# Half of a 31-tap depthwise convolution moved from the vector engine to float32 matmuls with diagonal matrices, in a two-block transformer kernel

## The chip, the cores and the metric

The kernel runs on one core of one Trainium2 chip. A core has five engines that work side by side and wait for each other by semaphores: TensorE (PE, with its weight loads PEld), VectorE (DVE), ScalarE (ACT), GpSimd (POOL) and SyncE (SP), which issues most of the transfers. The metric is the device time of one execution in microseconds (us); lower is better. Each engine takes its instructions strictly in the order in which they stand in its own list.

## The reference

The input is one sequence of 256 positions with 1024 channels, all in float32. A first block has two layers. Each layer has a hybrid mixer and a feed-forward part; the first layer's is dense, the second layer's is a mixture of 8 experts of which 2 are used per position. A second block (grouped attention, a linear recurrence and a dense feed-forward) follows. The part that the change touches is the convolution branch of the hybrid mixer:

```python
def hybrid_mixer(x, cos, sin, lambda_init, w_in, w_o, conv_dw, conv_dw_b, conv_ln_g, conv_ln_b, conv_pw, ...):
    proj = x @ w_in
    p_conv, p_q, p_k, p_v, p_dn, p_z, p_b, p_a = split_projection(proj)
    c_lin, c_gate = jnp.split(p_conv, 2, axis=-1)
    c = c_lin * jax.nn.sigmoid(c_gate)
    c = depthwise_conv(c, conv_dw) + conv_dw_b      # 256 channels, 31 taps, centred
    c = jax.nn.silu(layer_norm(c, conv_ln_g, conv_ln_b))
    y_conv = c @ conv_pw
    ...
    y_diff = differential_attention(...)            # 4 heads, two softmax maps each
    y_dn = gated_deltanet_bidir(...)                # chunked delta rule, both directions
    return jnp.concatenate([y_conv, y_diff, y_dn], axis=-1) @ w_o
```

The 256 convolution channels lie as two halves of 128, one channel per partition, with the 256 positions along the free axis.

## The kernel before, in words

The work comes in this order, with times read from the profiled execution: mixer of layer 0 (0 to about 226 us), dense feed-forward of layer 0 (226 to 405), mixer of layer 1 (405 to about 650), mixture of experts (650 to about 1600), second block (1600 to the end). Within a mixer, four generators (convolution `c`, attention `a`, delta rule `d`, gates `g`) are stepped in the order of a string (`ORDER`); a tile scheduler then sets the order of each engine's list from that and from its own dependency rules, so an edit in one generator can shift instructions of the others.

Large matmuls are done in three passes: a weight tile `raw` is cast by ACT to a high part `wH` (L173), the rest `wL = raw - wH` is made by DVE or POOL (L175), and PE multiplies three combinations (L179, L180, L181). Smaller matmuls run directly in float32.

Weights come in by `load` (L158): 2 MB into a `raw` buffer of 16 KB per partition. Outside the mixture `RAWS` such buffers are used in turn, from the pool `wp`, so a load waits until the tile that was last in its buffer has been split to the end. In the mixture there are `RAWS` buffers in `wp` and `MORE` in the mixture's own pool `mp`, whose memory the mixer uses before; a buffer in `mp` can be loaded only when the mixer's tiles there are done.

In the convolution branch, `cp` is the padded input of both halves (float32, tag `cv`), `tw` the 31 taps of a half (one per channel) and `acc` the result. For each half ACT makes the centre tap with the bias (L851), and DVE adds the 30 others, one instruction of 128x256 for each tap (L855), each reading and writing `acc`. The branch that has GpSimd in it is not taken, since `TAPS` is 2 and there are two halves. Later, L871 to L894 make the branch's layer norm and its pointwise projection; L871 is a float32 matmul of 128x128 by 128x256.

Other lines that the text names: L510 and L514 (ACT and DVE, the short convolution of the delta rule, tile `cq`), L518 (its silu, DVE), L562 (DVE, product of the delta rule's matrices, needs L557 of PE), L737 and L750 (PE, the delta rule's solve), L231 (ACT copies out of PSUM), L917 to L922 (DVE, rotary embedding), L946 (PE, attention scores), L950 to L963 (softmax), L185 (PE, transposes), L894 (PE, pointwise projection of the convolution branch).

Of the kernel before, what the change touches and what calls it, by code (L numbers as in the profile page):

```python
# [13 lines left out]
AF = mybir.ActivationFunctionType  # L14
OP = mybir.AluOpType
# [5 lines left out]
P = 128  # L21
# [1 line left out]

ORDER = ("ddggddddcaadacgadadaacdadd", "ddggdcddddaagadaacaacdddad")
PATS = (("G", "G", "", "G", "VVG", "VG"), ("VG", "", "G", "G", "VG", "G"))
TAPS = 2

STEPS = "R mb E B3 RT ET bk kd qd szg rot0 rot1 vv pT qdT wT qkT Q2 oc".split()
ENGS = ("VVVGGVGVGGAAAAAAAAA", "VGVVVVVGGGAAAAAAVVA")
# [8 lines left out]

WIDE = 192

MORE = 3
RAWS = 4
KT = D // P
ALPHA = 4.0 ** 0.25
LN_EPS = 1e-5
# [61 lines left out]
class K:  # L107
    def __init__(self, tc, ctx, a):
# [9 lines left out]

        self.raws = [(self.wp, RAWS)]
        self.cst = []  # L120
# [704 lines left out]
    def conv_branch(self, raw, xH, xL, pp, yH, yL, layer):  # L825
        V, A, G, T = self.V, self.A, self.G, self.T
        cb = []
        raw = raw()
        for u in range(2):
            b = self.bank()  # L830
            self.proj_T2(b, raw[:, :, u * 256:u * 256 + 256], xH, xL, pat=PATS[layer][4])
            cb.append(b.rearrange("p (j s) -> p j s", j=2))
        w, wb, g, lb = pp[:, 0:62], pp[:, 62:64], pp[:, 64:66], pp[:, 66:68]
        cv = lambda n=512: self.wk(n, "cv", 3).rearrange("p (j s) -> p j s", j=2)

        hg = self.sm([P, 4], "hg", 1)
        G.tensor_scalar(w, w, 0.5, None, op0=OP.mult)
        G.tensor_scalar(hg, pp[:, 64:68], 0.5, None, op0=OP.mult)
        pw = pp[:, 98:610].rearrange("p (k f) -> p k f", k=2)
        G.tensor_scalar(pw, pw, 0.5, None, op0=OP.mult)  # L840
        th = cv()
        A.activation(th, cb[1], AF.Tanh, scale=0.5)
        cp = cv(572)
        G.memset(cp, 0.0)
        V.scalar_tensor_tensor(cp[:, :, 15:271], th, 1.0, cb[0], op0=OP.add, op1=OP.mult)
        acc = cv()
        yield
        prod = self.wk(1024, "t32", 1).rearrange("p (k s) -> p k s", k=4)
        for j in range(2):
            tw = w[:, j * 31:j * 31 + 31]  # L850
            A.activation(acc[:, j], cp[:, j, 15:271], AF.Identity, scale=tw[:, 15:16], bias=wb[:, j:j + 1])  # L851
            if j < TAPS:
                for k in range(31):
                    if k != 15:
                        V.scalar_tensor_tensor(acc[:, j], cp[:, j, k:k + 256], tw[:, k:k + 1], acc[:, j], op0=OP.mult, op1=OP.add)  # L855
            else:
                for k0, n in ((0, 4), (4, 4), (8, 4), (12, 3), (16, 4), (20, 4), (24, 4), (28, 3)):

                    win = cp[:, j, k0:k0 + 256]
                    win = bass.AP(tensor=win.tensor, offset=win.offset, ap=[win.ap[0], [1, n], [1, 256]])  # L860
                    G.tensor_tensor(prod[:, :n], win, tw[:, k0:k0 + n, None].to_broadcast([P, n, 256]), OP.mult)
                    while n > 1:
                        h = n // 2
                        G.tensor_tensor(prod[:, :h], prod[:, :h], prod[:, n - h:n], OP.add)
                        n -= h
                    G.tensor_tensor(acc[:, j], acc[:, j], prod[:, 0], OP.add)
        yield

        b = self.bank()
        for j in range(2):  # L870
            T.matmul(b[:, 0:256], lhsT=self.c("ones"), rhs=acc[:, j], start=j == 0, stop=j == 1)  # L871
        V.scalar_tensor_tensor(acc, b[:, None, 0:256].to_broadcast([P, 2, 256]), -1.0 / 256, acc, op0=OP.mult, op1=OP.add)
        sq = cv()
        A.activation(sq, acc, AF.Square)
        for t in range(2):
            for j in range(2):
                T.matmul(b[:, t:t + 1], lhsT=sq[:, j, t * P:(t + 1) * P], rhs=self.c("ones")[:, 0:1], start=j == 0, stop=j == 1)
        rs = self.sm([P, 2], "crs", 1)
        V.tensor_copy(rs, b[:, 0:2])
        self.rsqrt(rs, rs, 1.0 / 256, LN_EPS)  # L880
        dg = self.wk(256, "cv", 3)
        for t in range(2):
            ts = slice(t * P, (t + 1) * P)
            V.tensor_scalar(dg[:, ts], self.c("ident"), rs[:, t:t + 1], None, op0=OP.mult)
            T.matmul(b[:, ts], lhsT=self.c("ones"), rhs=dg[:, ts], start=True, stop=True)
        V.tensor_tensor(acc, acc, b[:, None, 0:256].to_broadcast([P, 2, 256]), OP.mult)
        th, u = cv(), cv()
        for j in range(2):
            A.activation(th[:, j], acc[:, j], AF.Tanh, scale=hg[:, j:j + 1], bias=hg[:, 2 + j:3 + j])
            A.activation(u[:, j], acc[:, j], AF.Identity, scale=g[:, j:j + 1], bias=lb[:, j:j + 1])  # L890
        V.scalar_tensor_tensor(u, th, 1.0, u, op0=OP.add, op1=OP.mult)
        for f in range(2):
            for k in range(2):
                T.matmul(b[:, f * 256:f * 256 + 256], lhsT=pw[:, k, f * P:(f + 1) * P], rhs=u[:, k], start=k == 0, stop=k == 1)  # L894
        v = b.rearrange("p (f s) -> p f s", f=2)
        self.split(v, None, yH[:, 0:2], yL[:, 0:2])
# [467 lines left out]
    def moe(self, xn):  # L1364
# [3 lines left out]
        self.raws = [p.tile([P, 4096], F32, tag="raw", name=f"raw{n}x{i}", bufs=n) for p, n in (  # L1368
            (self.wp, RAWS), (self.mp, MORE)) for i in range(n)]
        self.chunk = 0  # L1370
# [8 lines left out]
        def part(r):  # L1379
# [3 lines left out]
            def ap(c, j):  # L1383
                if r not in regs:
# [11 lines left out]
                     xnH, xnL, pl, cmp_, xn, lambda: most.append(nc.values_load(idi[0:1, 7:8], min_val=0, max_val=S)))  # L1396
        self.raws = [(self.wp, RAWS)]
        ahead = self.block2_loads(0, RAWS)
        gb = self.xp.tile([P, 2, D], F32, tag="xTL", name="gb", bufs=1)
        for i in range(2):  # L1400
            A.dma_start(gb[:, i], a["ln"][1, 2 + i].partition_broadcast(P))

        self.raws = [(self.mp, MORE)]
        with self.tc.If(most[0] > P):
            self.experts([([(part(r), [(0, r, s)])], 1.0, alone) for r, s in (
                (0, P), (1, WIDE), (2, P), (3, P), (4, 64), (5, 64), (6, 64), (7, 64))], xnH, xnL, pl, cmp_, xn)
        self.raws = [(self.wp, RAWS)]
        g2 = self.row(a["rows2"][0], "yH")
# [25 lines left out]
    def block2_in(self, xn, xH, xL, ahead):  # L1434
# [9 lines left out]
        yH, yL = self.xT_tiles("b2y")  # L1444
        left = self.block2_loads(RAWS, 4)
        raws = lambda g: [r for n, r in ahead + left if n == g]
# [362 lines left out]
```

## Time and profile before

| | |
|---|---|
| time, median of 3 runs | 1973.8 us (1965.64 to 1977.03) |
| time of the profiled execution | 1976.9 us |
| span of the profiled execution | 1975.1 us |
| mean granted clock of TensorE | 0.944 of full speed |
| PE busy | 1815.8 us, 92% of the span |
| DVE busy | 1198.0 us, 61% |
| ACT busy | 835.3 us, 42% |
| POOL busy | 201.6 us, 10% |

The span goes from the first to the last instruction of the trace; 1.8 us of the execution lie around it. Busy time is the time in which an engine had an instruction under way. The granted clock is 1.0 at 2.4 GHz and 0.5 at 1.2 GHz, and a value between is a mean over a stretch.

### The profile page before, as it was taken

How to read it: one execution, taken by the hardware profiler on the slowest of the kernel's cores; microseconds unless marked ns; L12 is line 12 of the kernel's file. 1: busy time of each engine (PE TensorE's matmuls, PEld its weight loads, DVE VectorE, ACT ScalarE, POOL GpSimd, SP SyncE). 2: the span in 40 equal slices, each digit the busy share in tenths (PEclk: the TensorE clock that was granted, in tenths of full speed). 3: DMA queues.
4: the chain of work that ended last, by engine and by line, in shares of the span. 5: the costliest groups of instructions: out<-in, count | busy, mean ns of one | idle time of the engine just before them, and what ended most of it. 6: DMA issues, size and time to landing. Idle time of an engine off the chain costs nothing. (4 is left out here: it accounts for less than half of the span.)

```text
span 1975.1 us, 28866 instructions
## 1 busy us (share of the span) xinstructions
PE 1815.8 (92%) x11670; PEld 1401.1 (71%) x11670; DVE 1198.0 (61%) x1717; ACT 835.3 (42%) x1176; POOL 201.6 (10%) x128
## 2 busy tenths in 40 slices
PE   7788999987788999999999999999999968899998
PEld 6766899976667776666666666666666637789997
DVE  6896654479975854545454644344544557757776
ACT  3234344443333544434443433334443526545554
POOL 4252200033323000000000000000000013010000
PEclk9788899998879899999999999999999988799999
DMA  7220435363203789999999778888999944144550
GB/s 287 107 107 23 176 145 213 129 228 118 95 14 129 298 364 421 421 421 377 410 400 405 294 297 306 303 339 312 362 413 411 407 162 166 43 151 159 197 187 22
DMA packets 61773, 484.83 MB, mean 245 GB/s; under 512 B 7232, under 2 KB 7872, under 8 KB 10688
## 3 DMA queue, kind: packets, MB, share of 16 engines
q1 hardware_dynamic: 59184, 475.75, 61.6%
q10 hardware_dynamic: 2448, 7.17, 1.1%
q8 instruction: 93, 1.52, 0.3%
q14 instruction: 48, 0.39, 0.1%
HBM read 481.84 MB, written 1.05 MB: 244 GB/s over the span
## 5 line engine op out<-in xcount | busy, mean ns | idle before, releaser
L173 ACT CAST wH<-raw 128x1024 fp32r<-128x1024 f32 (+1 forms) x224 | 232.5, 1049 | 292.2 <-PE mm L180 160.7
L175 DVE TENSOR_TENSOR wL<-raw,wH 128x1024 fp32r<-128x1024 f32 (+1 forms) x174 | 213.2, 1233 | 154.7 <-ACT wH L173 154.5
L175 DVE TENSOR_TENSOR wL<-raw4x,wH 128x1024 fp32r<-128x1024 f32 x192 | 227.5, 1222 | 63.6 <-ACT wH L173 56.8
L173 ACT CAST wH<-raw4x 128x1024 fp32r<-128x1024 f32 x192 | 194.0, 1050 | 40.7 <-PE acc L181 24.2
L175 DVE TENSOR_TENSOR wL<-raw3x,wH 128x1024 fp32r<-128x1024 f32 x144 | 171.2, 1222 | 47.0 <-ACT wH L173 44.9
L179 PE MATMUL mm<-wH,g 128*128 128x512 f32 x448 | 179.2, 400 | 0.0
L180 PE MATMUL mm<-wL,g 128*128 128x512 f32 x448 | 177.1, 395 | 0.0
L181 PE MATMUL mm<-wH,g 128*128 128x512 f32 x448 | 175.7, 392 | 0.0
L179 PE MATMUL acc<-wH,hH 128*128 128x512 f32 x408 | 156.2, 407 | 20.7 <-ACT wH L173 20.0
L180 PE MATMUL acc<-wL,hH 128*128 128x512 f32 x408 | 165.0, 405 | 8.2 <-DVE wL L175 8.2
L181 PE MATMUL acc<-wH,hL 128*128 128x512 f32 x408 | 162.0, 398 | 0.0
L173 ACT CAST wH<-raw3x 128x1024 fp32r<-128x1024 f32 x144 | 145.7, 1050 | 25.3 <-PE acc L181 13.0
L1250 PE MATMUL mm<-raw4x,gx 128*64 128x256 f32 x1280 | 145.3, 381 | 0.0
L175 POOL TENSOR_TENSOR wL<-raw,wH 128x1024 fp32r<-128x1024 f32 x50 | 125.8, 2526 | 123.7 <-ACT wH L173 123.3
L191 POOL TENSOR_TENSOR sm_brs<-sm_brs,half_neg 128x1 f32<-128x1 f32 x8 | 12.1, 1517 | 1179.7 <-PE mm L312 974.9
L1250 PEld LDWEIGHTS mm<-raw4x,gx 128*64 128x64 f32 x1280 | 89.3, 137 | 49.1 <-issue 7.1
L1326 ACT ACTIVATE ff<-mm 128x256 f32<-128x256 f32 x35 | 13.5, 385 | 250.7 <-PE mm L1250 250.7
L179 PEld LDWEIGHTS acc<-wH,hH 128*128 128x128 f32 x408 | 76.6, 191 | 47.8 <-ACT wH L173 26.4
L179 PE MATMUL mm<-b2yH,wH 128*128 128x256 f32 x384 | 109.5, 286 | 0.0
L180 PE MATMUL mm<-b2yL,wH 128*128 128x256 f32 x384 | 109.5, 285 | 0.0
L181 PE MATMUL mm<-b2yH,wL 128*128 128x256 f32 x384 | 109.3, 285 | 0.0
L1250 PE MATMUL mm<-raw3x,gx 128*64 128x256 f32 x960 | 108.9, 382 | 0.0
(528 smaller groups left out, 3754.7 us busy)
## 6 DMA issues: line engine op xcount, KB each, us to landing
raw4x<-in_moe_dram SPq DMA_DIRECT2D x192, 1024.0 KB, 8.5
raw3x<-in_moe_dram SPq DMA_DIRECT2D x144, 1024.0 KB, 8.7
raw<-in_ffn_dram SPq DMA_DIRECT2D x33, 2048.0 KB, 7.7
raw<-in_w_in_dram SPq DMA_DIRECT2D x13, 2048.0 KB, 9.4
raw<-in_w_o_dram SPq DMA_DIRECT2D x4, 2048.0 KB, 7.6
raw<-in_w_out_dram SPq DMA_DIRECT2D x2, 2048.0 KB, 8.9
raw<-in_w_in_dram SPq DMA_DIRECT2D x3, 1024.0 KB, 4.8
row<-in_ln_dram ACTq DMA_DIRECT2D x6, 512.0 KB, 3.6
```

Source lines behind the costliest of these rows:

```text
L173: self.A.copy(H, src)
L175: (eng or self.V).tensor_tensor(L, src, H.bitcast(F32), OP.subtract)
L179: self.T.matmul(out, lhsT=lh, rhs=rh, start=start, stop=False)
L180: self.T.matmul(out, lhsT=lh, rhs=rl, start=False, stop=False)
L181: return self.T.matmul(out, lhsT=ll, rhs=rh, start=False, stop=stop)
L191: return self.G.tensor_tensor(out, out, self.half_neg.to_broadcast([P, n]), OP.pow)
L1250: T.matmul(out[i * 64:i * 64 + 64], lhsT=lhsT, rhs=rhs[:, i * n:i * n + n], start=start, stop=stop)
L1326: A.activation(sn[-1], b[:, 0:256], AF.Silu)
```

## The change

For the second half of the channels (`j == 1`) the centre tap on ACT and the 30 taps on DVE go. In their place ACT makes 31 diagonal matrices of 128x128 (the identity scaled by one tap per channel, `dgk`, L859 of the new file), PE multiplies each by the shifted window of `cp` in float32 and adds all 31 in one PSUM bank (L860), and ACT moves the bank out and adds the bias (L861). The first half stays as it was. The 31 matrices take 16 KB per partition; one load buffer moves from `wp` to `mp` (`RAWS` 4 to 3, `MORE` 3 to 4).

```diff
-TAPS = 2
...
-MORE = 3
-RAWS = 4
+MORE = 4
+RAWS = 3
...
         acc = cv()
         yield
-        prod = self.wk(1024, "t32", 1).rearrange("p (k s) -> p k s", k=4)
         for j in range(2):
             tw = w[:, j * 31:j * 31 + 31]
-            A.activation(acc[:, j], cp[:, j, 15:271], AF.Identity, scale=tw[:, 15:16], bias=wb[:, j:j + 1])
-            if j < TAPS:
+            if j == 0:
+                A.activation(acc[:, j], cp[:, j, 15:271], AF.Identity, scale=tw[:, 15:16], bias=wb[:, j:j + 1])
                 for k in range(31):
                     if k != 15:
                         V.scalar_tensor_tensor(acc[:, j], cp[:, j, k:k + 256], tw[:, k:k + 1], acc[:, j], op0=OP.mult, op1=OP.add)
             else:
-                for k0, n in ((0, 4), (4, 4), (8, 4), (12, 3), (16, 4), (20, 4), (24, 4), (28, 3)):
...
-                    G.tensor_tensor(acc[:, j], acc[:, j], prod[:, 0], OP.add)
+
+                o = self.bank()[:, 0:256]
+                for k in range(31):
+                    d = self.wk(P, "dgk", 31)
+                    A.activation(d, self.c("ident"), AF.Identity, scale=tw[:, k:k + 1])
+                    T.matmul(o, lhsT=d, rhs=cp[:, j, k:k + 256], start=k == 0, stop=k == 30)
+                A.activation(acc[:, j], o, AF.Identity, bias=wb[:, j:j + 1])
         yield
```

The scheduler places the new instructions. The lines of the new file stand one lower up to the branch and five lower behind it (L946 of before is L941 there, L562 is L561).

PE's list in the mixer of layer 0, behind the run of 96 three-pass matmuls of the value projection (`mm_1075` and `mm_1076` are its last banks); before, the scores of the first two heads (`aT`) come next:

```order
L179 MATMUL mm_1076<-wH_1127,x0H 128x512
L180 MATMUL mm_1076<-wL_1128,x0H 128x512
L181 MATMUL mm_1076<-wH_1127,x0L 128x512
L946 MATMUL mm_1218<-aT_984,aT_895 128x256
L946 MATMUL mm_1219<-aT_984,aT_895 128x256
L946 MATMUL mm_1218<-aT_984,aT_895 128x256
L946 MATMUL mm_1219<-aT_984,aT_895 128x256
L185 MATMUL acc_1286<-cst_4_126,cq_256 128x128 x4
```

The same place in the changed kernel, with the 31 products (`dgk`) of which the first two and the last are shown:

```order
L179 MATMUL mm_1076<-wL_1128,x0H 128x512
L180 MATMUL mm_1076<-wH_1127,x0L 128x512
L860 MATMUL mm_1177<-cv_815,dgk_1178 128x256
L860 MATMUL mm_1177<-cv_815,dgk_1181 128x256
...
L860 MATMUL mm_1177<-cv_815,dgk_1268 128x256
L941 MATMUL mm_1281<-aT_984,aT_895 128x256
L941 MATMUL mm_1282<-aT_984,aT_895 128x256
L941 MATMUL mm_1281<-aT_984,aT_895 128x256
L941 MATMUL mm_1282<-aT_984,aT_895 128x256
L184 MATMUL acc_1349<-cst_4_126,cq_256 128x128 x4
```

All 31 stand in one piece ahead of the scores and of everything behind them. In layer 1 they stand behind the value products of the first attention heads (L970 of before, L965 there) and ahead of the next heads' scores.

DVE's list in the mixer of layer 1, from the scaling of the delta rule's operands (`s`, `cq`) to the first softmax maxima (`sm_amx`), before:

```order
L707 TENSOR_TENSOR cq_4802<-s_3873,sm_bG_4791 128x1024
L714 TENSOR_TENSOR s_4772<-s_4772,cst_368_3740 128x1024
L855 SCALAR_TENSOR_TENSOR cv_4098<-cv_4095,pp_3744,cv_4098 128x256 x19
L562 TENSOR_TENSOR s_4772<-acc_4805,s_4772 128x8x64
L562 TENSOR_TENSOR s_4772<-acc_4806,s_4772 128x8x64
L855 SCALAR_TENSOR_TENSOR cv_4098<-cv_4095,pp_3744,cv_4098 128x256 x2
L950 TENSOR_REDUCE sm_amx_4831<-mm_4825 128x2
```

The same place in the changed kernel:

```order
L706 TENSOR_TENSOR cq_4865<-s_3936,sm_bG_4854 128x1024
L713 TENSOR_TENSOR s_4835<-s_4835,cst_399_3803 128x1024
L853 SCALAR_TENSOR_TENSOR cv_4161<-cv_4158,pp_3807,cv_4161 128x256 x3
L561 TENSOR_TENSOR s_4835<-acc_4868,s_4835 128x8x64
L561 TENSOR_TENSOR s_4835<-acc_4869,s_4835 128x8x64
L945 TENSOR_REDUCE sm_amx_4894<-mm_4888 128x2
```

Of the 19 taps ahead of L562 three are left, and the taps between the softmax steps behind it are gone.

ACT's list at the start of layer 0, from the short convolution of the first bank (`cq`) on, before (`raw_138` is the third weight part):

```order
L510 ACTIVATE cq_256<-acc_141,pp_132 128x256
L457 ACTIVATE sm_nega_299<-rows_134 128x8
L907 ACTIVATE sm_l_821<-sm_l_821 128x2
L510 ACTIVATE cq_256<-acc_141,pp_132 128x256
L173 CAST wH_605<-raw_138 128x1024
L517 ACTIVATE t_268<-cq_256 128x512
```

The same place in the changed kernel, up to the second L509:

```order
L509 ACTIVATE cq_256<-acc_141,pp_132 128x256
L456 ACTIVATE sm_nega_299<-rows_134 128x8
L859 ACTIVATE dgk_1178<-cst_4_126,pp_132 128x128
...
L859 ACTIVATE dgk_1208<-cst_4_126,pp_132 128x128
L902 ACTIVATE sm_l_821<-sm_l_821 128x2
L859 ACTIVATE dgk_1211<-cst_4_126,pp_132 128x128
L509 ACTIVATE cq_256<-acc_141,pp_132 128x256
L859 ACTIVATE dgk_1214<-cst_4_126,pp_132 128x128
```

Twelve of the 31 scalings now stand ahead of the second L509, and six more stand between it and the cast of `raw_138`.

The order of SP's loads stays as it was, apart from one part of layer 1's input weights, which goes behind that layer's small tables. What each load waits for moves by one buffer: with three buffers it waits for the last split of the tile three loads earlier, where it was four.

## Rows read from the trace of the kernel before

**Rows 1.** The page's section 1: busy us, share of the span, instructions.

```profile
PE 1815.8 (92%) x11670; PEld 1401.1 (71%) x11670; DVE 1198.0 (61%) x1717; ACT 835.3 (42%) x1176; POOL 201.6 (10%) x128
```

**Rows 2.** Both mixers: length, busy PE, PEld, DVE, ACT, POOL, then clock, DMA.

```profile
0.00:226.00 226.00, 181.87 (x1498) 152.07 (x1498) 173.51 (x324) 82.32 (x144) 79.86 (x48) 0.86 0.35 133
405.00:650.00 245.00, 200.00 (x1595) 164.42 (x1594) 193.60 (x387) 85.00 (x151) 85.07 (x51) 0.85 0.29 110
```

**Rows 3.** What PE waited for, 0 to 226 us: total, times, longest.

```profile
PE mm L185 <- DVE at L922: 7.9, 2, 7.5
```

**Rows 4.** The same, 405 to 650 us.

```profile
PE mm L185 <- DVE at L922: 14.1, 3, 11.7
```

**Rows 5.** Timeline of DVE, layer 0: start, duration, line, names, shape, count.

```profile
100.96 17.36 DVE L855 SCALAR_TENSOR_TENSOR cv<-cv,pp,cv 128x256 f32<-128x256 f32 x22
...
122.23 8.00 DVE L855 SCALAR_TENSOR_TENSOR cv<-cv,pp,cv 128x256 f32<-128x256 f32 x20
```

**Rows 6.** Timeline of DVE in layer 1.

```profile
539.80 17.50 DVE L855 SCALAR_TENSOR_TENSOR cv<-cv,pp,cv 128x256 f32<-128x256 f32 x19
557.21 1.28 DVE L562 TENSOR_TENSOR s<-acc,s 128x512 f32<-128x512 f32 x2
```

**Rows 7.** L871 and L894, layer 1: ns min/median/max, first and last start.

```profile
L871 PE MATMUL mm<-cv,cst x4: 379/379/382, 594.4 to 595.1; 128*128 128x256 f32 x4
...
L894 PE MATMUL mm<-cv,pp x8: 634/634/796, 604.3 to 607.5; 128*128 128x256 f32 x8
```

**Rows 8.** Windows of the mixers, columns as in group 2.

```profile
144.00:148.00 4.00, 3.75 (x31) 2.56 (x30) 4.00 (x7) 0.00 (x0) 3.31 (x3) 0.60 0.00 0
...
156.00:160.00 4.00, 4.00 (x44) 3.55 (x45) 3.94 (x8) 1.54 (x3) 0.00 (x0) 0.50 0.30 111
...
564.00:571.00 7.00, 6.61 (x71) 5.57 (x67) 5.39 (x16) 4.48 (x13) 0.00 (x0) 0.55 0.23 75
...
578.00:592.00 14.00, 13.79 (x118) 10.07 (x118) 7.42 (x27) 5.26 (x20) 0.00 (x0) 0.51 0.00 1
```

**Rows 9.** Timeline of PE in layer 0, the wait ahead in brackets.

```profile
140.48 1.14 PE L946 MATMUL mm<-aT,aT 64*128 64x256 f32 x8
142.78 0.66 PE L185 MATMUL acc<-cst,cq 128*128 128x128 f32 x4 [1.17 <-DVE cq L518]
...
144.30 0.73 PE L557 MATMUL acc<-qkT,qkT 64*64 64x64 f32 x16 [0.25 <-DVE sz L481]
...
149.31 2.08 PE L737 MATMUL acc<-s,s 64*64 64x64 f32 x64 [0.63 <-DVE s L562]
...
154.92 0.62 PE L185 MATMUL mm<-cst,at 128*128 128x128 f32 x2 [2.97 <-DVE at L963]
```

**Rows 10.** Timeline of PE in layer 1.

```profile
547.56 0.85 PE L557 MATMUL acc<-qkT,qkT 64*64 64x64 f32 x26
...
557.95 3.55 PE L737 MATMUL acc<-s,s 64*64 64x64 f32 x64 [6.58 <-DVE s L562]
563.64 0.91 PE L750 MATMUL acc<-s,cq 64*64 64x64 f32 x22 [2.13 <-ACT s L231]
```

**Rows 11.** Timeline of ACT at the start.

```profile
17.89 0.20 ACT L457 ACTIVATE sm_nega<-rows 128x8 f32<-128x8 f32 x1
...
20.25 0.47 ACT L510 ACTIVATE cq<-acc,pp 128x256 f32<-128x256 f32 x1 [0.19 <-DVE cq L514]
21.55 1.05 ACT L173 CAST wH<-raw 128x1024 fp32r<-128x1024 f32 x1 [0.83 <-DMA raw<-in_w_in_dram]
```

**Rows 12.** Timeline of DVE, dense feed-forward: a load's last split.

```profile
263.72 1.23 DVE L175 TENSOR_TENSOR wL<-raw,wH 128x1024 fp32r<-128x1024 f32 x1 [1.60 <-ACT wH L173]
```

**Rows 13.** Timeline of ACT, dense feed-forward: the first cast three loads later.

```profile
276.92 1.05 ACT L173 CAST wH<-raw 128x1024 fp32r<-128x1024 f32 x1 [1.44 <-issue]
```

**Rows 14.** The page's section 6: KB each, median us from issue to landing.

```profile
raw<-in_ffn_dram SPq DMA_DIRECT2D x33, 2048.0 KB, 7.7
```

**Rows 15.** A window early in the mixture, columns as in group 2.

```profile
692.00:696.00 4.00, 4.00 (x24) 2.28 (x25) 0.51 (x1) 0.00 (x0) 0.00 (x0) 0.71 0.00 0
```

More of the change, by code (lines that the diff above doesn't have):

```diff
@@ L856, in conv_branch @@
             else:
-                for k0, n in ((0, 4), (4, 4), (8, 4), (12, 3), (16, 4), (20, 4), (24, 4), (28, 3)):
[L859 to L865, printed above, removed]
-                    G.tensor_tensor(acc[:, j], acc[:, j], prod[:, 0], OP.add)
+                o = self.bank()[:, 0:256]
[4 more added lines that the diff above has]
+                A.activation(acc[:, j], o, AF.Identity, bias=wb[:, j:j + 1])
         yield
```

## The prediction

> **What bounds the kernel now.** First comes the page's table of engines: PE is busy 92% of the span, DVE 61% [rows 1]. That is a mean over stages, so the next view cuts the span by stage. In the mixers PE is busy only 181.9 of 226 us and 200.0 of 245 us, and DVE almost as long, 173.5 and 193.6 us [rows 2]. The two take turns there: PE waits some 45 us in each mixer, mostly for DVE. The view of waits says for what. In both mixers the longest wait is for the rotary embedding, 7.5 us in layer 0 [rows 3] and 11.7 us in layer 1 [rows 4]. The timelines then show what DVE does ahead of it, and that decides which waits the change can touch.
>
> The taps stand in two groups. In layer 0, 22 of them run from 100.96 us, at 0.79 us each, and end where the 7.5 us wait ends; a further 20 run from 122.23, at 0.40 us each [rows 5]. In layer 1, 19 run from 539.80 to 557.30, at 0.92 us each, and PE then gets its operand [rows 6]. The scheduler put nearly all of the first half's taps ahead of the second half's, so those that go are the later ones. The long waits for the embedding lie behind taps that stay: in layer 0, 25 stand ahead of it in the changed list and 26 before, in layer 1 one fewer. I count nothing for them.
>
> **What is added on PE.** 31 float32 products of 128x128 by 128x256 for each mixer. L871 is the same product: its 2 products leave 4 records, which start from 594.4 to 595.1, so 0.23 us for a record [rows 7]. 31 products are 62 records, 62 x 0.23 = 14.4 us at full clock. At half clock L894 gives (607.5 - 604.3)/7 = 0.46 us a record, so 28.3 us [rows 7]. That is the upper bound; I take full clock, since in layer 0 the products follow a long run of dense matmuls, and 1 us more in layer 1, where they follow a stretch at clock 0.55 [rows 8]. PE takes its list in order, and in layer 0 all 31 stand in one piece between that run and the scores. Before, the scores followed the run without a wait, at 140.48 [rows 9]: PE wasn't idle there, so the whole 14.4 us go on the path.
>
> **What layer 0 gets back.** The 20 taps at 122.23 ran beside dense matmuls and held nothing up; their 8.0 us are free time on an engine that wasn't waited for. Those interleaved with the short convolution were waited for: PE waited 1.17 us for L518 at 142.78 [rows 9]. In the changed kernel L518 has some 14 us more, so this wait goes, and so do the 0.25 and 0.63 us behind it [rows 9]. The 2.97 us for L963 [rows 9] are the softmax chain of scores, maximum, exponential and scaling. That chain starts only behind the 31 products, but DVE will have cleared its other work by then; I take half, 1.5 us. Behind the small matmuls the clock stood at 0.60 from 144 to 148 us, which cost 0.4 x 4 = 1.6 us [rows 8]; with a dense run just ahead I count that as gained. Sum for layer 0: 14.4 - 1.2 - 0.9 - 1.5 - 1.6 = +9.2 us.
>
> **What layer 1 gets back.** PE waits 6.58 us for L562, which stands behind the 19 taps [rows 6, 10]. What L562 needs of PE, L557, is done at 548.4 [rows 10]; with 3 taps ahead DVE is there by 542.6 (3 x 0.92 us from 539.80), so L562 runs at 548.4 and the wait goes: -6.6. L737 took 3.55 us after the idle time [rows 10] and 2.08 us in layer 0 [rows 9]: -1.5. The 2.13 us for ACT's copy behind it [rows 10] shrink with the taps between the softmax steps, but ACT now makes the exponentials in the same place: -0.6. Five taps fewer lie ahead of two short waits before: -1.2. Against the products' 14.4 + 1.0 that leaves 15.4 - 9.9 = +5.5 us.
>
> **What is added on ACT.** 31 scalings of 128x128 for each mixer; no row has one. The nearest above is L510 at 128x256, 0.47 us, the nearest below L457 at 128x8, 0.20 us [rows 11]; consecutive ones overlap by 0.1 us, so between 0.10 and 0.37 us each, and I take 0.26, the middle. In layer 0 twelve stand ahead of the second L510. From 18.1 us (17.89 + 0.20) they take 3.1 us to 21.2, where L510 started at 20.25; six more push the cast from 21.55 to 23.3 [rows 11]. Behind them lies the start of the delta rule, on which PE soon waits. I count +1.2 us, between 0 and 3. The other scalings are scattered where ACT waits for PE: it is busy 82 of 226 us [rows 2]. The two copies out of PSUM replace two centre taps of the same size.
>
> **What the moved buffer does.** Each load outside the mixture now waits for a split one load later. In the dense feed-forward a tile's last split ends at 264.95 and the first cast of the tile three loads on starts at 276.92 [rows 12, 13]: 12.0 us, against 7.7 us from issue to landing [rows 14]. The 4.3 us left hide the change there; the second block's feed-forward loads in the same pattern. Should landing take over 12 us, each of some 11 chunks would wait. At the start of the mixture one buffer fewer can be filled early. From 692 to 696 us its transfers stand still (DMA share 0.00 [rows 15]) which I read as all seven buffers being full, and the missing load fits there. I take 0, and up to +3 for both.
>
> **Sum.** 9.2 + 5.5 + 1.2 + 0 = +15.9 us on the profiled execution's 1976.9, so 1992.8. The median of the runs is 1973.8, 3.1 us below that execution; on it the sum gives 1989.7, and I predict 1989. Half a per cent, 9.9 us, is about what a measurement of this kernel can tell from no change. This case's own span is +10 to +23.
>
> **The clock, a rival within half a per cent.** Small matmuls let the granted clock fall to about half even where PE had no wait: 0.51 from 578 to 592 us with PE busy 13.79 of 14 us, besides 0.55 from 564 to 571 and 0.50 from 156 to 160 [rows 8]. These three cost 0.49 x 14 + 0.45 x 7 + 0.50 x 4 = 12.0 us against full clock. If the 31 dense products keep the clock at 2.4 GHz through what follows them, those 12.0 us come back, and the sum is 15.9 - 12.0 = +3.9, time 1978. Against it: the dense run of layer 0 ends at 140.5 us, and the clock falls in the window from 144 to 148 all the same [rows 8]. The Trainium skill says the same of the cause: in "TensorE: Matmul & The Clock Gate", Part 1, the gate passes half or all of the pulses by how busy PE has just been. By that rule the sum would be +3.9, were the products near enough to all four stretches. The trace agrees on the two levels, but no row shows how far one dense run carries. 0.22.
>
> **The other side: faster.** If the products were hidden, only the gains would be left: -(1.2 + 0.9 + 1.5 + 1.6) - 9.9 + 1.2 = -13.9, time 1960. For it: each mixer holds some 45 us of PE waiting, and DVE is full for long stretches. It decides whether PE would have waited anyway where the 31 stand, so whether the list around them still waits for DVE once they are through. Against it: no wait stood there [rows 9], and the 7.5 and 11.7 us holes lie earlier in the lists, where nothing can be moved into them. 0.11.
>
> **Loads, further out.** If two transfers at a time take 14 us to land, 11 chunks lose 2 us each: +22 on the sum, time 2012. For it: transfers share the DMA engines. Against it: the 7.7 us are a median of 33 loads, with two often under way. 0.09.
>
> **How the numbers follow.** The forecast has 0.58. Range 1974 to 2003: its lower end takes in the clock's case and half of the way to the faster one, its upper end half clock for one of the runs of products. Slower by over 0.5%: 0.49 of the forecast's 0.58 and the loads' 0.09, 0.58. Same: the remaining 0.09 and 0.21 of the clock's case, 0.30. Faster: 0.11 and 0.01, 0.12.
>
> **What would show it.** L860 as 62 records over 14 to 15 us, without waits inside, behind the dense run in layer 0, with the scores at 155 to 157 us; L562 (now L561) in layer 1 done within 2 us of L557, and no wait of 6.6 us ahead of L737; the waits for the embedding still near 7 and 11 us; the feed-forwards and the mixture as long as before (179 us from 226 to 405). The forecast is wrong if the records of L860 overlap closer than 0.23 us, if the clock stays at 1.0 where it was 0.5, if the waits for the embedding shrink by more than 2 us, or if casts in the feed-forwards begin to wait for loads.

## The result and the profile after

The changed kernel takes 1995.6 us, the median of 5 runs (1989.6 to 2000.7), against 1973.8 us before on the same chip (5 runs, 1965.6 to 1977.0): a ratio of 1.0115, 95% interval 1.0079 to 1.0151, slower. The profiled execution's span is 1996.4 us, 21.3 us above that of before. The page's section 1 of the changed kernel answers to [rows 1]; its two windows of the mixers answer to [rows 2].

```profile
PE 1846.0 (92%) x11794; PEld 1429.4 (72%) x11794; DVE 1166.5 (58%) x1657; ACT 852.2 (43%) x1238; POOL 198.4 (10%) x128
```

```profile
0.00:226.00 226.00, 187.38 (x1515) 157.50 (x1516) 146.97 (x278) 84.93 (x168) 67.82 (x44) 0.86 0.31 116
405.00:650.00 245.00, 208.83 (x1681) 176.60 (x1680) 166.51 (x314) 94.03 (x179) 79.37 (x46) 0.87 0.30 109
```

PE has 30.2 us more to do, DVE 31.5 us less: the work went from the engine that had time left to the one that is 92% busy. To see where it shows, compare the instants at which the same instructions run in the two traces. The table gives for three places how much later they lie than in the trace of before, in us; the text calls this the shift. The last gate product of layer 0 (L694 of before, L693 after) ended at 113.3 us; the layer norm behind layer 0's mixer (DVE L273, L272) ended at 225.0, that behind layer 1's mixer at 636.1. The last columns are the granted clock from 150 to 200 us and the ratio to before. Behind the second layer norm the changed kernel loses 2 us more in the mixture and then nothing.

| kernel | gate product, layer 0 | end of mixer 0 | end of mixer 1 | mixer 1 alone | clock 150:200 | ratio, 95% interval |
|---|---|---|---|---|---|---|
| before | 0 | 0 | 0 | 0 | 0.86 | 1 |
| changed | +6.5 | +14.7 | +19.3 | +4.6 | 0.94 | 1.0115 (1.0079 to 1.0151) |
| buffers_alone | -0.1 | -0.4 | +0.4 | +0.8 | 0.84 | 1.0006 (0.9986 to 1.0026) |
| no_scalings | -0.5 | +9.6 | +14.2 | +4.6 | 0.90 | other data |
| no_scalings_old_buffers | -0.2 | +10.0 | +17.9 | +7.9 | 0.90 | other data |
| two_products | -0.2 | +11.8 | +3.4 | -8.4 | 0.67 | other data |
| scalings_on_gpsimd | +12.7 | +24.1 | +35.8 | +11.7 | 1.00 | 1.0206 (1.0180 to 1.0233) |
| scalings_later | +1.1 | +11.3 | +15.8 | +4.5 | 0.90 | 1.0127 (1.0110 to 1.0144) |
| products_other_bank | +46.7 | +21.0 | +30.4 | +9.4 | 0.83 | 1.0165 (1.0140 to 1.0189) |
| products_ahead_of_projections | +23.1 | +27.4 | +26.9 | -0.5 | 0.69 | 1.0113 (1.0089 to 1.0138) |
| one_pass_products | +7.2 | +5.6 | +0.3 | -5.3 | 0.88 | 1.0016 (0.9998 to 1.0033) |
| one_pass_scalings_later | +0.4 | +9.5 | -1.6 | -11.1 | 0.69 | 1.0032 (1.0016 to 1.0048) |
| one_pass_layer_1 | +0.2 | -0.1 | -11.3 | -11.2 | 0.83 | 0.9987 (0.9970 to 1.0003) |
| one_pass_layer_1_ahead | -0.6 | -0.6 | -10.8 | -10.2 | 0.86 | 0.9973 (0.9954 to 0.9992) |

A shift is that of one execution against one. Single executions of the kernel before lie between 1962.4 and 1980.4 us, and two of the kernels, `no_scalings` and `no_scalings_old_buffers`, whose lists are the same on every engine up to the mixture, differ by 3.7 us at its start: so much chance is in a shift. That difference is one of the granted clock, 0.87 against 0.78 from 540 to 580 us (0.09 x 40 = 3.6 us). The ratios come from all runs. In the three kernels with other data the second half's taps are all 1, or most are left out; the mixture, whose work hangs on its input, then lasts 1008 to 1009 us longer, and of these kernels only what lies ahead of it is read.

The products themselves, on PE's timeline in layer 0 of the changed kernel (start, duration, line, names, shape, count), where [rows 9] had the scores at 140.48:

```profile
144.64 0.40 PE L180 MATMUL mm<-wH,x0L 128*128 128x512 f32 x1
144.87 13.55 PE L860 MATMUL mm<-cv,dgk 128*128 128x256 f32 x62
158.36 1.14 PE L941 MATMUL mm<-aT,aT 64*128 64x256 f32 x8
...
165.67 0.41 PE L184 MATMUL mm<-cst,at 128*128 128x128 f32 x2 [1.05 <-DVE at L958]
```

62 records in 13.55 us, 0.22 us each, without a wait on either side: nothing hid them. What hid behind them are the short waits: the 1.17, 0.25 and 0.63 us of [rows 9] are gone and the 2.97 us for the softmax are 1.05. In layer 1, where [rows 10] had a wait of 6.58 us ahead of L737:

```profile
560.28 0.85 PE L556 MATMUL acc<-qkT,qkT 64*64 64x64 f32 x26
...
564.01 1.37 PE L736 MATMUL acc<-s,s 64*64 64x64 f32 x38
...
577.33 3.39 PE L860 MATMUL mm<-cv,dgk 128*128 128x256 f32 x10
...
580.66 0.60 PE L860 MATMUL mm<-cv,dgk 128*128 128x256 f32 x2
...
581.21 10.96 PE L860 MATMUL mm<-cv,dgk 128*128 128x256 f32 x50
...
594.03 1.02 PE L749 MATMUL acc<-s,cq 64*64 64x64 f32 x26
594.98 0.44 PE L759 MATMUL acc<-zero 128*128 128x128 f32 x2
```

The wait is gone, and L736 comes 6.1 us late instead of the 12.7 us by which the work ahead of it was late. But 26 matmuls of L749 and the start of the delta rule's recurrence (L759) now stand behind the products, at 594.98 instead of 571.7 us: 23.3 us late. That chain then ends last. The view of waits (total, times, longest) of PE, 0 to 226 us and then 405 to 650, shows it in the wait for the gated output `sz`, which was 0.4 and 0.3 us before:

```profile
PE mm L184 <- DVE at L917: 8.0, 3, 5.4
...
PE acc L184 <- DVE sz L816: 2.5, 1, 2.5
...
PE mm L184 <- DVE at L917: 12.6, 2, 11.0
PE acc L184 <- DVE sz L816: 4.7, 1, 4.7
```

The other lines answer to [rows 3] and [rows 4]: the waits for the embedding are still there, 5.4 and 11.0 us.

One more place shows how the shift comes and goes inside a mixer: the convolution branch's layer norm on PE (L871 of before, L866 after). In layer 0 the shift is 4.5 us ahead of the products, 17.9 at the scores behind them, 8.9 at L866 and 14.7 at the mixer's end. In layer 1 it is 12.7 us ahead of L556, 10.8 at L866 and 19.3 at the end. So the stretch between the products and L866 gives much back, and the stretch behind L866 takes part of it again: 5.8 us in layer 0 and 8.5 in layer 1, and the same within 0.2 us in the traces of `no_scalings`, `no_scalings_old_buffers` and `scalings_later`. Two things behind L866 are longer than before: the wait for `sz`, by 2.1 and 4.4 us, and the time at half clock. The windows (columns as in [rows 2]) are, before, scores to L871 in layer 0, L871 to the end of mixer 0, L871 to the end of mixer 1; then the same in the changed kernel:

```profile
140.50:179.60 39.10, 33.67 (x429) 26.36 (x429) 31.93 (x78) 17.78 (x53) 13.99 (x9) 0.87 0.12 42
179.60:225.00 45.40, 35.78 (x189) 28.42 (x189) 27.63 (x46) 16.25 (x24) 15.99 (x9) 0.87 0.25 93
594.40:636.10 41.70, 36.69 (x228) 29.80 (x227) 20.77 (x44) 16.12 (x24) 15.72 (x11) 0.92 0.29 106
```

```profile
158.40:188.50 30.10, 27.89 (x389) 21.48 (x389) 21.22 (x64) 15.23 (x48) 4.02 (x4) 1.00 0.12 37
188.50:239.70 51.20, 39.94 (x230) 31.78 (x228) 27.93 (x48) 16.34 (x24) 16.00 (x9) 0.82 0.23 83
605.20:655.40 50.20, 44.39 (x309) 36.66 (x310) 22.32 (x52) 16.05 (x23) 15.72 (x11) 0.83 0.24 88
```

By estimate from these rows, the clock gives back up to 0.13 x 39.1 = 5.1 us between the scores and L866 in layer 0, and behind L866 it takes up to 3.3 us more than before there (0.18 x 51.2 against 0.13 x 45.4) and up to 5.2 us more in layer 1 (0.17 x 50.2 against 0.08 x 41.7). "Up to", because PE also waits in these windows.

### The profile page after: what moved, and what is told of

Same layout as the page of the kernel before. It is cut to its first block, busy times and chain, and to the rows that moved or that the text cites. A ratio compares the mean times of both kernels' runs of the same rounds, so it can differ in the third digit from the quotient of the medians.

```text
span 1996.4 us, 29122 instructions
## 1 busy us (share of the span) xinstructions
PE 1846.0 (92%) x11794; PEld 1429.4 (72%) x11794; DVE 1166.5 (58%) x1657; ACT 852.2 (43%) x1238; POOL 198.4 (10%) x128
## 3 DMA queue, kind: packets, MB, share of 16 engines
HBM read 481.84 MB, written 1.05 MB: 242 GB/s over the span
## 4 chain that ended last, share of the span: by engine, by line
issue 49%; PE 19%; DVE 6%; ACT 1%; POOL 0%; POOLq 0%; DVEq 0%; ACTq 0%
PE mm L179 3%; PE mm L178 3%; PE mm L180 3%; PE acc L178 2%; PE acc L179 2%; PE acc L180 2%; PE mm L184 1%; DVE cv L853 1%; PE mm L860 1%; DVE wL L174 1%; PE mm L1669 1%; DVE t L604 0%; PE mm L1646 0%; DVE xn L272 0%; DVE cq L513 0%
## 5 line engine op out<-in xcount | busy, mean ns | idle before, releaser
L174 DVE TENSOR_TENSOR wL<-raw4x,wH 128x1024 fp32r<-128x1024 f32 x188 | 223.0, 1221 | 64.4 <-ACT wH L172 55.3
L172 ACT CAST wH<-raw4x 128x1024 fp32r<-128x1024 f32 x188 | 189.9, 1050 | 34.4 <-PE acc L180 19.0
L174 DVE TENSOR_TENSOR wL<-raw3x,wH 128x1024 fp32r<-128x1024 f32 x148 | 175.4, 1221 | 45.4 <-ACT wH L172 40.0
L172 ACT CAST wH<-raw3x 128x1024 fp32r<-128x1024 f32 x148 | 149.7, 1050 | 31.0 <-PE acc L180 19.0
L1245 PE MATMUL mm<-raw4x,gx 128*64 128x256 f32 x1312 | 150.2, 385 | 0.0
L1245 PE MATMUL mm<-raw3x,gx 128*64 128x256 f32 x928 | 104.8, 381 | 0.0
```

The source lines that it names most:

```text
L172: self.A.copy(H, src)
L174: (eng or self.V).tensor_tensor(L, src, H.bitcast(F32), OP.subtract)
L1245: T.matmul(out[i * 64:i * 64 + 64], lhsT=lhsT, rhs=rhs[:, i * n:i * n + n], start=start, stop=stop)
```

## The experiments

**The parts of the change.** The first four kernels run one part of the change each, to see which of them costs the time. `buffers_alone` is the kernel before with

```diff
-MORE = 3
-RAWS = 4
+MORE = 4
+RAWS = 3
```

> The kernel before with nothing changed but the two counts of load buffers (three instead of four common ones, four instead of three of the mixture's own); the taps stay on VectorE. Theory (the products' place in TensorE's row costs the time; the buffer costs only what the trace of the changed kernel lost between 691 and 858 us): 2 to 3 us slower than before, all of it in the mixture, and both mixers unchanged within 1 us. Rival (the buffer also holds up the loads of the first mixer, where the changed kernel lost 4 us between 97 and 118 us): 6 us or more slower, with the loss before 226 us.

Ratio 1.0006 (0.9986 to 1.0026), mixers unchanged within 0.8 us: neither the rival nor even the theory's 2 to 3 us show. The 2 us that the changed kernel lost in the mixture are not the buffer's by any view here; in this kernel that stretch came 3 us earlier than before, so they are of the size by which executions differ.

`no_scalings` is the changed kernel with

```diff
-                    d = self.wk(P, "dgk", 31)
-                    A.activation(d, self.c("ident"), AF.Identity, scale=tw[:, k:k + 1])
+                    d = self.c("ident")
```

> The changed kernel without the 62 scalings of the identity on ScalarE: every product takes the identity itself, so the second half's 31 taps are all 1. The products, their place and the buffers stay. Theory: the scalings cost only the 1.5 to 2.3 us at the start and perhaps part of the 4 us between 97 and 118 us, so that it stays 15 to 19 us slower than before. Rival (the scalings' 24 us on ScalarE hold up the casts of weights that TensorE waits for): 10 us or less slower than before.

The mixers end 14.2 us late, not 19.3. All 5 us come from layer 0. So by the shift the truth lies just below the theory's range and well above the rival's. The three traces' casts of weights on ACT say how. First the changed kernel: the scalings and the cast at the start, which answer to [rows 11], and two later casts.

```profile
18.54 3.32 ACT L859 ACTIVATE dgk<-cst,pp 128x128 f32<-128x128 f32 x11
...
24.25 1.04 ACT L172 CAST wH<-raw 128x1024 fp32r<-128x1024 f32 x1
...
96.08 1.05 ACT L172 CAST wH<-raw 128x1024 fp32r<-128x1024 f32 x1 [0.27 <-PE mm L180]
...
108.57 1.05 ACT L172 CAST wH<-raw 128x1024 fp32r<-128x1024 f32 x1 [3.30 <-PE mm L180]
```

The same two casts without the scalings:

```profile
84.52 1.04 ACT L172 CAST wH<-raw 128x1024 fp32r<-128x1024 f32 x1 [0.46 <-PE mm L180]
101.23 1.05 ACT L172 CAST wH<-raw 128x1024 fp32r<-128x1024 f32 x1 [3.66 <-PE mm L180]
```

The start is only 2 us late. But with 31 more instructions in ACT's list the scheduler put one cast of weights behind two instructions of other steps (L234 and L516) that had stood behind it, and it runs 11.6 us later. The load that needs its buffer goes out at 99.08 us instead of 94.29, and the next cast stands at 108.57 instead of 101.23.

`no_scalings_old_buffers` is `no_scalings` with the buffers of before, `two_products` has in addition

```diff
-                for k in range(31):
+                for k in (0, 30):
```

> As no_scalings (the second half's taps are all 1), and with the load buffers as before: four common ones, three of the mixture's own. What is left of the change is the 62 products, their evacuation and the taps that VectorE no longer does. Theory: 2 to 3 us less than no_scalings, by the mixture's part, so 13 to 16 us slower than before; the products' 27 us less the waits that they release. Rival (the buffer matters in the mixers too): 6 us or more below no_scalings.

> As no_scalings_old_buffers, and with 2 products (the first and the last tap) in place of the 31 in each mixer, so that 29 taps of the second half are left out. It shows what VectorE's freed time is worth when TensorE pays next to nothing for it. Theory (the products stand in line on a TensorE that waits for little, so their 26 us come off almost whole, and in layer 1 the delta rule's chain behind them also starts earlier): 8 to 14 us faster than before, 24 to 28 us below no_scalings_old_buffers. Rival (the taps were hidden behind TensorE's work, and a further wait takes the place of each one removed): within 4 us of before.

With the old buffers the mixers end 17.9 us late, 3.7 more than with the new ones where 2 to 3 less were expected; as the lists are the same and the clock makes the difference, this tells nothing but the size of chance. `two_products` ends them 14.5 us earlier than that, not 24 to 28. It did what the theory said in layer 1 (-8.4 us) and the opposite in layer 0: +11.8 us, with 2 products, where 31 cost +10.0. In layer 0 PE's clock is what differs. The window from 152 to 182 us (length, busy PE, PEld, DVE, ACT, POOL, then granted clock, DMA share, GB/s), in `two_products`, in `no_scalings_old_buffers`, in the kernel before and in the changed one:

```profile
152.00:182.00 30.00, 29.65 (x240) 21.72 (x240) 12.59 (x43) 10.46 (x32) 1.45 (x2) 0.52 0.05 19
```

```profile
152.00:182.00 30.00, 27.95 (x384) 21.29 (x383) 20.48 (x62) 15.21 (x48) 3.33 (x3) 1.00 0.11 37
```

```profile
152.00:182.00 30.00, 26.00 (x314) 20.46 (x314) 22.07 (x64) 13.38 (x40) 3.83 (x5) 0.89 0.11 36
```

```profile
152.00:182.00 30.00, 28.02 (x338) 21.73 (x336) 17.01 (x48) 12.12 (x39) 3.32 (x3) 1.00 0.12 37
```

With the products PE runs this stretch at 2.4 GHz, in `two_products` almost all of it at 1.2 GHz; 0.89 - 0.52 of 30 us are 11.1 us, nearly the whole loss of `two_products` in layer 0. So in this execution the taps that left DVE gave 8.4 us in layer 1, and in layer 0 a clock that fell took back what they may have given. That the missing products made the clock fall is not shown.

**The scalings' place.** Two kernels leave the products and move the scalings: to GpSimd (`A.activation(...)` becomes `G.tensor_scalar(d, self.c("ident"), tw[:, k:k + 1], None, op0=OP.mult)`), and in layer 0 behind the last cast issued before:

```diff
-        self.A.copy(H, src)
+        self.cast = self.A.copy(H, src)
...
-                    A.activation(d, self.c("ident"), AF.Identity, scale=tw[:, k:k + 1])
+                    with self.tc.issue_after(self.cast.ins) if layer == 0 else nullcontext():
+                        A.activation(d, self.c("ident"), AF.Identity, scale=tw[:, k:k + 1])
```

> The changed kernel with one edit: the 62 scalings of the identity are issued to GpSimd instead of ScalarE; what is computed stays. Theory (the scalings cost 5 us of the first mixer through ScalarE's row: 2 us at the start, and 3 us because a cast of weights then stands 11 us later, at 96 instead of 85 us, and with it the next load): 3 to 7 us below the changed kernel, so 15 to 20 us slower than before. Rival (the diagonals cost as much wherever they are made, since GpSimd has half of the weights' low parts in its row): 21 us or more slower than before.

> The changed kernel with one edit: in layer 0 the 31 scalings may only follow the last cast of weights that was issued before the convolution's taps, so that by the order ScalarE does them behind its casts of the attention's weights (some 109 us) and not between 18 and 37 us; layer 1 and what is computed stay. Theory (in layer 0 the scalings cost 5 to 7 us by their place in ScalarE's row, not by their 12 us): 4 to 7 us below the changed kernel, 15 to 19 us slower than before. Rival (the last diagonals then come too late for the products, or TensorE's 13.6 us hide what the start loses): within 2 us of the changed kernel, 21 us or more slower than before.

On GpSimd they cost far more, as the rival said: ratio 1.0206, some 40 us. GpSimd's timeline, and PE's longest wait for it in the first 60 us:

```profile
18.58 19.34 POOL L859 TENSOR_SCALAR dgk<-cst,pp 128x128 f32<-128x128 f32 x31
37.90 0.36 POOL L475 TENSOR_SCALAR sm_ng<-rows 128x64 f32<-128x64 f32 x1
38.23 2.33 POOL L174 TENSOR_TENSOR wL<-raw,wH 128x1024 fp32r<-128x1024 f32 x1
...
PE mm L180 <- POOL wL L174: 16.7, 1, 16.7
```

The low part of a weight tile stands behind all 31, and the start loses 13 us. So this run says nothing of ACT's part; `scalings_later` does. Its trace has the cast back at 86.07 and the gate product at +1.1 instead of +6.5:

```profile
86.07 1.04 ACT L172 CAST wH<-raw 128x1024 fp32r<-128x1024 f32 x1 [0.46 <-PE mm L180]
...
132.04 2.45 ACT L860 ACTIVATE dgk<-cst,pp 128x128 f32<-128x128 f32 x8
```

3.4 us of the 5.1 stay gained to the end of the mixer. But the ratio, 1.0127 (1.0110 to 1.0144), is some 25 us above before, the rival's figure, and lies inside the interval of the changed kernel, which was timed on another occasion. So the trace shows where the scalings cost, and the total does not show that moving them pays.

**The products' place and their price.** `products_other_bank` takes the sum's bank from the pool of the states (`self.bank("acc")`), `products_ahead_of_projections` has in addition

```diff
-ORDER = ("ddggddddcaadacgadadaacdadd", "ddggdcddddaagadaacaacdddad")
+ORDER = ("ddggddddcacadagadadaacdadd", "ddggdcddddacagadaaaacdddad")
```

and `one_pass_products` keeps the place and changes the type:

```diff
+                cr = self.wk(286, "cpr", 1).bitcast(F32R)
+                A.copy(cr, cp[:, j])
                 for k in range(31):
-                    d = self.wk(P, "dgk", 31)
+                    d = self.wk(P, "dgk", 28).bitcast(F32R)
...
-                    T.matmul(o, lhsT=d, rhs=cp[:, j, k:k + 256], start=k == 0, stop=k == 30)
+                    T.matmul(o, lhsT=d, rhs=cr[:, k:k + 256], start=k == 0, stop=k == 30)
```

> The changed kernel with one edit: the products' sum lies in a bank of the other pool (the one of the states), which is free earlier; by the order, 8 of layer 0's 31 products then stand where TensorE waits for the attention's normalised rows (5.4 us), 23 behind the projections; layer 1's place stays. Theory (a product costs nothing where TensorE waits, and its full time in line): 3 to 4 us below the changed kernel, 18 to 20 us slower than before. Rival (the 8 products come too late for that wait, or the bank is then missing to the delta rule): within 1 us of the changed kernel or slower.

> As products_other_bank, and the order of the mixers' steps has the convolution's second step earlier in both layers: by the order, all 31 products then stand before the attention's last projections, and in layer 1 where TensorE waits 11 us for the normalised rows; the first half's 30 taps on VectorE come earlier with them. Theory (in layer 1 the products cover that wait and the delta rule's chain no longer stands behind them): 8 to 14 us slower than before. Rival (VectorE's taps, now ahead of the attention's rows, make these as much later as the products' place gives): 20 us or more slower than before.

> The changed kernel with the 62 products in the one-pass type that the projections use (float32r) instead of float32: the diagonals and the second half's input are rounded to it, with one more copy on ScalarE in each mixer, and 28 diagonals' buffers instead of 31 for room. Theory (TensorE's time in line is the price): from the projections' 512 columns in 0.23 us, 31 products of 256 columns take 3 to 4 us instead of 13.6, so some 20 us below the changed kernel, within 5 us of before. Rival (the clock: with the products short, the stretch behind them falls to the half clock, as with two products, where layer 0 lost 12 us): 8 to 14 us slower than before.

`products_other_bank` fell: ratio 1.0165, and layer 0 6 us worse than the changed kernel. Five products ran ahead of the wait for the embedding, which ended where it did in the changed kernel (125.1 us), so they were free; three more came behind it, and the projections after them start some 1 us later than in the changed kernel. But the bank then stays taken until the last one, and the delta rule's L494, at 110.11 us before, gets its own only behind them. In layer 1 the delta rule's solve (L736) comes behind the products too, and the wait for `sz` grows to 7.0 us. PE's timeline in layer 0:

```profile
116.50 2.32 PE L860 MATMUL acc<-cv,dgk 128*128 128x256 f32 x10
125.14 1.08 PE L184 MATMUL mm<-cst,at 128*128 128x128 f32 x4 [6.31 <-DVE at L917]
126.02 2.77 PE L860 MATMUL acc<-cv,dgk 128*128 128x256 f32 x6
...
145.83 10.10 PE L860 MATMUL acc<-cv,dgk 128*128 128x256 f32 x46
155.86 1.13 PE L941 MATMUL mm<-aT,aT 64*128 64x256 f32 x8
156.93 1.98 PE L494 MATMUL acc<-s,cst 128*128 128x512 f32 x4
```

`products_ahead_of_projections` split by layer: layer 1 came out at -0.5 us, 5 better than the changed kernel, while layer 0 lost 27.4 us; the total, 1.0113, is the rival's and that of the changed kernel. Of the theory for layer 1 only one half holds. The wait for the embedding is as long as in the changed kernel, 11.0 us up to 524.3 us, and the products stand behind it, at 556.28, so they cover nothing of it; what is gone is the wait for `sz` at the mixer's end. `one_pass_products` has 3.87 us where the changed kernel has 13.55, in layer 1 5.4 (570.83 to 576.24) where it has 14.8, 19.1 us less in all, and a ratio of 1.0016 (0.9998 to 1.0033): 19 us back, as the theory said. TensorE's time in line was the price. PE's timeline in layer 0:

```profile
145.42 3.87 PE L862 MATMUL mm<-cpr,dgk 128*128 128x256 f32 x31
```

**A version that beats both.** Layer 1 wins 5.3 us with short products and layer 0 does not, so the next kernels keep what pays. `one_pass_scalings_later` joins the two edits above; `one_pass_layer_1` has `if j == 0 or layer == 0:` in place of `if j == 0:`, so that layer 0's 60 taps stay on DVE; `one_pass_layer_1_ahead` adds the other bank and layer 1's order of `products_ahead_of_projections`.

> As one_pass_products (diagonals and the second half's input rounded to float32r, 28 buffers of diagonals), with layer 0's scalings placed as in scalings_later. Theory (one_pass_products lost 5.6 us in layer 0, of which the scalings' place is 5 to 7, and won 5.3 us in layer 1): 3 to 8 us faster than before. Rival (with 28 buffers the last scalings wait for the first products, or the half clock behind the short products takes it back): within 3 us of before, or slower.

> As one_pass_products, but layer 0 keeps all 60 taps on VectorE as before; only layer 1's second half has diagonals and 31 one-pass products. Theory (layer 1's 5.3 us are won there and do not hang on layer 0): 3 to 8 us faster than before. Rival (part of the 5.3 us is one execution's chance, or the mixture takes it back): within 2 us of before.

> As one_pass_layer_1 (the second half's taps of layer 1 alone as one-pass products with rounded operands), with the products' sum in the other pool's bank and layer 1's order of steps as in products_ahead_of_projections, so that they stand ahead of the attention's last projections; layer 0 as before. Theory (what is left of the cost in layer 1 is the delta rule's chain behind the products: one_pass_layer_1 still shows 4.7 us of waiting for its gate at the mixer's end, and products_ahead_of_projections shows none): 4 to 10 us faster than before. Rival (the first half's 30 taps, ahead of the attention's and the delta rule's work on VectorE, bring back what the place gives): within 3 us of before, or slower.

`one_pass_scalings_later` is slower, 1.0032 (1.0016 to 1.0048), against the theory. Its layer 0 starts on time (+0.4) and ends at +9.5 us, with the clock at 0.69 from 150 to 200 us; against 0.86 before, 0.17 x 50 = 8.5 us are the clock's. That is the rival's second half, in the layer in which `one_pass_products` had kept 0.88. `one_pass_layer_1` is 0.9987 (0.9970 to 1.0003), between the two. Its trace ends layer 1 11.3 us early, of which the runs confirm at most 6: some 3 us were won ahead of L556 already, where the change has put no products yet, with a clock of 0.91 from 455 to 548 us against 0.85 before. It still shows the wait at the mixer's end:

```profile
PE acc L184 <- DVE sz L816: 4.7, 1, 4.7
```

With the products ahead of the projections that wait is 0.3 us:

```profile
PE acc L184 <- DVE sz L816: 0.3, 1, 0.3
```

and the time is 1963.1 us against 1971.0, a ratio of 0.9973 (0.9954 to 0.9992): faster than before by some 5 us (2 to 9 by the interval), and by some 28 us than the changed kernel, which was timed on another occasion. That the place ahead of the projections adds to this is not shown: the interval overlaps that of `one_pass_layer_1`, and in the traces mixer 1 gains 10.2 us against its 11.2. The products stand there at a mean clock of 0.66 (526 to 536 us) and take 6.24 us instead of 3.87 at 1.00, and mixer 1 still ends early:

```profile
528.16 6.24 PE L862 MATMUL acc<-cpr,dgk 128*128 128x256 f32 x31
```

## Why the prediction was right, and which terms were off

Slower by 15.9 us was forecast and 21.3 us came, by the spans; the time, 1995.6, is 7 us above the forecast of 1989 and inside the range. The main mechanism was right: the products stand in line on PE and cost their full time, only short waits hide behind them in layer 0, and one long one goes in layer 1. That the two mixers came out within 1 us of their sums is luck in good part: in each, more came back behind the products than the sum had, and a loss at the mixer's end that the sum didn't have took the surplus away. Three of the forecast's four signs of being wrong came, each by a little: records of L860 0.22 us apart, a clock of 1.00 where it was 0.50 (156 to 160 us), and 2.1 us off a wait for the embedding.

- **The products in layer 0, +9.2 without the scalings:** +9.6 and +10.0 without them. They took 13.55 us where 14.4 were taken (62 x 0.23 is 14.3). The 0.23 came from rounded instants: PE's timeline has the four records of L871 in 1.03 us, (1.03 - 0.38)/3 = 0.22 each. Between the scores and L866 9.0 us came back (17.9 - 8.9) where the sum has 5.2. The waits in it hold: three short ones gone, and the softmax's wait shrunk by 1.9 where 1.5 were taken. The clock was taken at 1.6 us and is worth up to 5.1. Behind L866 5.8 us went again, a term that the sum lacks.
- **The scalings on ACT, +1.2, between 0 and 3:** 5.1 us (14.7 - 9.6). This is the term that was mis-sized. The spacing was guessed near enough: 11 in 3.32 us are (3.32 - 0.39)/10 = 0.29 us each where 0.26 were taken. The Trainium skill has the better guess, on the page "ScalarE: Activation LUTs", section "What ACT_TABLE_LOAD costs": 186 ns and 0.833 ns a column, 93 ns more for a pointer operand, and successive ones overlap by 93 ns, so by estimate 386 ns each, 293 ns apart. The trace agrees, with a median of 389 ns. What failed is the step that looked for their cost only where they stand, up to 23 us: some 4 us (6.5 - 2.3) arise behind 96 us, through the one cast that changed its place in ACT's list, far below the rows that the forecast read.
- **Layer 1, +5.5:** +4.6 in this execution, +7.9 in the one with old buffers. The 6.6 us for L562 came back to the tenth (12.7 - 6.1). The products took 14.8 us of the 15.4 taken, from 577.33 to 592.2, the first ten at 0.33 us each. From L556 to L866 16.7 us came back (12.7 + 14.8 - 10.8) where the sum has 9.9, and 2.0 more ahead of L556. Not in the sum was what went behind L866, 8.5 us: the delta rule's chain, which started 23.3 us late, cost 4.4 us there (`sz`, 4.7 us instead of 0.3), and the clock up to 5.2. How much of the 16.7 each wait and the clock gave is not shown.
- **Loads and buffer, 0 to +3:** right by `buffers_alone`. The dense feed-forward, from 226 us to the start of layer 1's gates at 455, lost 0.3 us; the rival of late loads falls with it.
- **The waits for the embedding stay:** 5.4 and 11.0 us instead of 7.5 and 11.7. Layer 0's shrank by 2.1 us, a little over the 2 that the forecast allowed, because PE came to it later; that hid 2 of the 6.5 us by which PE was late there. The 22 taps of [rows 5] end at 118.3 us and not with the wait, which lasts to 120.8; no term hangs on it.
- **The clock's rival:** its mechanism is there, its conclusion is not. From 152 to 182 us the changed kernel has 1.00 where before had 0.89, which is worth 0.11 x 30 = 3.3 us and is part of the +9.6. But the clock falls all the same, later: from 190 to 213 us it is 0.70, and behind L866 both mixers have less of it than before, 0.82 against 0.87 and 0.83 against 0.92. In layer 1 it is 0.50 at the first products (577 to 579 us). The Trainium skill, in "TensorE: Matmul & The Clock Gate", Part 1, lets the clock hang on how busy the engine has just been; the trace agrees on the two levels, but the stretch at 0.52 had PE busy 29.65 of 30 us, more than the one at 1.00, so the profile's busy share does not tell which it will be.
- **The rival of hidden products:** falls by `one_pass_products`, in which 19.1 us less of products gave 19 us back.

What stays open is why the clock falls for some 30 us in `two_products` (0.52 from 152 to 182 us) and `one_pass_scalings_later` (0.69 from 150 to 200), and for less in the kernel before, though much the same matmuls stand behind 150 us. No run here set it apart from the small differences in their order and their waits. Open with it is why the stretch behind L866 has less clock in the changed kernel.

## What to carry to other kernels

Work moved from an engine with idle time to the busiest one cost its full duration here, because no wait stood exactly where it landed in that engine's list; so look for one there, price the work by the cheapest form that will do (here one pass instead of float32, 3.87 us against 13.55) and look at what is then queued behind it. Read the whole list of each engine that gets new instructions, not just the rows beside them: 31 cheap ones moved a cast that stood 70 us away. And take a gain per layer: with short products the traces show 5 to 11 us won in one mixer and 6 to 10 lost in the other, and only a kernel that kept the one was faster, by some 5 us. Last, check a sum that comes out right part by part: here two errors of 4 to 9 us in each mixer cancelled.

## What was not expected of the hardware

Less work on TensorE made a stretch slower: with 29 products fewer in layer 0 the granted clock from 152 to 182 us was 0.52 instead of 1.00, and the mixer ended no earlier than with all of them (+11.8 against +10.0 us, closer than chance in a shift can tell apart). And GpSimd took 0.60 us for a scaling of 128x128 that ScalarE starts every 0.29 us (31 in 19.34 us there, against 11 in 3.32).
